# Recurrence gates as fp32r products, a later attention transpose and new pacing prices in a two-layer encoder trunk

## The chip, the cores and the metric

One core of one Trainium2 chip runs the whole kernel in one launch. The metric is device time in microseconds; a measurement is the median of several runs. The engines are named as the profile names them: PE (matrix products), DVE (vector), ACT (activation), POOL (GpSimd) and SP (which issues most transfers). They run side by side, each takes its own instructions in order, and they meet through semaphores.

## The reference

Two layers work on a sequence of 512 tokens of width 1024. A layer first mixes tokens: the normalised input goes through one combined projection and feeds three branches (a gated 128-block mixing, a sparse attention with 128 selected keys per query, and a gated linear recurrence). The branches are projected, gated and summed, then projected once more and added to the stream. A convolutional feed-forward part follows in the same way. The change concerns the recurrence's two gates and the order of work in the attention:

```python
xc = causal_dwconv(xb, conv_w, conv_b)
xg = xc.reshape(bsz, seq, LRU_BLOCKS, LRU_BLOCK_DIM)          # 8 blocks of 64 channels
r = jax.nn.sigmoid(jnp.einsum('bsnc,ncd->bsnd', xg, w_r).reshape(bsz, seq, LRU_WIDTH) + b_r)
i = jax.nn.sigmoid(jnp.einsum('bsnc,ncd->bsnd', xg, w_i).reshape(bsz, seq, LRU_WIDTH) + b_i)
log_a = -LRU_C * r * jax.nn.softplus(-lam)
a = jnp.exp(log_a)
b = jnp.sqrt(-jnp.expm1(2.0 * log_a)) * (i * xc)
h = scan(a, b)                                                 # h[t] = a[t] h[t-1] + b[t]
```

## The kernel before

Everything lies with channels on the 128 partitions and the 512 tokens along the row. A dense product is a **unit**: one weight tile of 128 x 1024 is loaded from HBM by SP, split into a high part (ACT, a copy that rounds to fp32r) and a low part (DVE, a subtraction), and multiplied in three fp32r products per 128 rows (`mm3`, line 163: high by high, high by low, low by high), so 24 matmuls of 512 columns. `Stream.conv` (line 197) splits weights up to five units ahead (`LA`), through six staging buffers. The order of the units is a fixed list (`unit_names`, line 40): four `lx` (recurrence input), four `qi` and one `ki` (selection), `v`, `lg`, `gv`, `gu`, the recurrence's branch, four pairs `k`, `q`, the other two branches, then the output projection `wo` and the feed-forward units. In layer 0 the first seven units are computed in the program's head, in layer 1 the first five in the tail of the layer before; `col` (line 428) then only hands their results over (`carry`).

Beside the units run background tasks, written as generators. After each unit the program calls `B.pump` (line 247); each call is a **slot**. A task that yields a negative number sleeps so many slots. Tasks marked `must` run in every slot that they are due; the others (selection, and the `low` modulation sums) run only while the counter `work["v"]` (priced DVE work) is under `work["pe"]` (priced PE work) plus 2. `cost_v`, `cost_g` and `cost_t` (lines 109 to 119) hold the prices. All this decides only the order in which instructions are issued; nothing is reordered at run time.

The recurrence is `lru` (line 625), a `must` task added after the four `lx` slots. It sleeps three slots in layer 0, two in layer 1, then per slot computes the gates of one tile of 128 channels: two fp32 matmuls of 512 columns with block-diagonal weights (two blocks of 64 channels) on the convolved tile `xc[t]`, two sigmoids on ACT. Then come exponentials, square root, scan, and four slots later the products that the recurrence's branch takes (`get_yc`, line 985). The convolved tile is made in `layer` (lines 824 to 832): one ACT instruction and three DVE instructions per tile.

In the same slots the `qi` units get a rotation (`rope`, line 556: two ACT copies, one DVE and two POOL operations) and are split (`split_qi`, line 839: ACT, POOL, ACT); `place_low` (line 846) then moves low parts to other partitions by four SP transfers per tile.

Attention (`attention`, line 727) is a `must` task with one step per slot and 12 groups of query blocks. At step n it transposes group n-2 on PE (`flip`), multiplies group n-3 with the values, divides group n-1 on DVE, and scores group n (matmul, DVE reduction, ACT exponential). A head's first score waits for four slots after its `q` unit, and each group for its selection mask `bias[i]` (two slots after `ready[i]`). The result `yb` is taken by the third branch through `get_yb` (line 1009), which drains all tasks.

Of the kernel before, what the change touches and what calls it, by code (L numbers as in the profile page):

```python
# [16 lines left out]
P = 128  # L17
D = 1024
# [50 lines left out]
def trunk_kernel(ctx: ExitStack, tc: tile.TileContext, x, cc, wt, wf, wm, wu, cp, rows, gmw, gmb, lruw, cst, out):  # L69
# [44 lines left out]
    def cost_g(op, a):  # L114
        if op == "tensor_tensor":
            work["v"] += size(a[0]) * 0.0008
# [508 lines left out]
    def lru(l, xc, lw, s84, wts, gl, res):  # L625
        rr, ii = [], []
        yield -3 if l == 0 else -2
        for t in range(4):
            for wi_, ob, lst in ((0, O_BR, rr), (1, O_BI, ii)):
                p = bank()  # L630
                mm(p, wts[wi_][:, t * P:(t + 1) * P], xc[t], True, True)
                o = S()
                act(o, p, AF.Sigmoid, bias=lw[:, ob + t:ob + t + 1])
                lst.append(o)
            if t < 3:
                yield -1
# [90 lines left out]
    def attention(qk, at, v, bias, ready, res):  # L727
# [51 lines left out]
        for n in range(len(groups) + 3):  # L779
            if 2 <= n < len(groups) + 2:  # L780
                for pr in groups[n - 2]:
                    flip(*pr)
            if n >= 3:
                for pr in groups[n - 3]:
                    values(*pr)
            if 1 <= n <= len(groups):
                for pr in groups[n - 1]:
                    divide(*pr)
            if n < len(groups):
                for hd, i in groups[n]:  # L790
                    while len(qk) <= hd or B.slot < at[hd] + 4 or i not in bias or B.slot < ready[i] + 2:
                        yield -1
                    score(hd, i)
            yield 1.0
            yield -1
# [20 lines left out]
    def layer(l):  # L816
        lw, bg2, s84 = par.pop(l)
        B.low.append(mods([(l, 2, ("G", 0)), (l, 4, ("A", 1)), (l, 3, ("B", 1))]))
# [190 lines left out]
        def get_yb():  # L1009
            B.drain()  # L1010
            return yb
# [88 lines left out]
    def rstd0(q):  # L1100
        ts(q, q, D * EPS, None, AD)
        return rsqrt(q)
# [29 lines left out]
    ys[3] = rstd0(sumsq_v(3))  # L1132
    ys[2] = rstd0(q2)
    scale0(3, V)
    scale0(2, A_)
# [82 lines left out]
def lay_out(a):  # L1218
# [48 lines left out]
    for l in range(DEPTH):  # L1267
# [3 lines left out]
        c[:, O_BR:O_BR + 4] = cols(a["lru_b_r"][l])  # L1271
        c[:, O_BI:O_BI + 4] = cols(a["lru_b_i"][l])
# [19 lines left out]
    lruw = np.zeros((DEPTH, 2, P, 4, P), f)  # L1292
    for i, n in enumerate(("lru_w_r", "lru_w_i")):
        w = a[n].reshape(DEPTH, 4, 2, 64, 64)
        for e in range(2):
            lruw[:, i, e * 64:(e + 1) * 64, :, e * 64:(e + 1) * 64] = w[:, :, e].transpose(0, 2, 1, 3)
# [45 lines left out]
```

## Time and profile before

| | us |
|---|---|
| median of 3 runs (1716.35 to 1716.80) | 1716.53 |
| the profiled execution, its own time | 1715.37 |
| its span, first to last instruction | 1713.6 |
| PE busy | 1682.9 (98%) |
| DVE busy | 1139.0 (66%) |
| ACT busy | 698.7 (41%) |
| POOL busy | 258.8 (15%) |

Times are from the start of the span. Matmuls overlap in the pipeline: a row says 0.39 us for one whose successor starts 0.23 us later, so the pace is read from starts, and an idle time that a row names is what was left after the modelled end. `L106` is the line of the wrapper through which the priced instructions are issued, `L144` and `L139` those of ACT's copies and activations, so tiles (`ps`, `s`, `wh`, `wl`) tell what an instruction is. `ps<-s,s` on PE is a product of two working tiles (gates, scores, values), `ps<-ks,s` a transpose, `ps<-hh,wh` and the like a unit.

### The profile page before, as it was taken

The page shows a single profiled execution, that of the slowest core. Times are in us where ns is not written, and L with a number is a line of the kernel's source. Part 1 is how long each engine was busy: PE and PEld are TensorE (multiplying, and loading weights), DVE is VectorE, ACT ScalarE, POOL GpSimd, SP SyncE. Part 2 cuts the span into 40 slices and gives each one's busy share as a digit, 9 for nine tenths or more (in the row PEclk, how much of TensorE's full clock was granted, in tenths as well). Part 3 has the DMA queues.
Part 4 walks back from the last instruction along what each step waited for, and adds up shares of the span by engine and source line. Part 5 has one row for each costly group of instructions (what it writes and reads, how often), then busy time and mean ns, then how long its engine had stood idle before and what let it go on. Part 6 is the DMA issues. An engine that isn't in the chain of part 4 may idle for free.

```text
span 1713.6 us, 20805 instructions
## 1 busy us (share of the span) xinstructions
PE 1682.9 (98%) x7900; PEld 1399.4 (82%) x7900; DVE 1139.0 (66%) x1687; ACT 698.7 (41%) x1074; POOL 258.8 (15%) x231
## 2 busy tenths in 40 slices
PE   7999998999999999999999999989999999999998
PEld 6788886888888888888897888877888988888886
DVE  7778999674567787453566889886455686445442
ACT  6774234342344433332346632343333343333331
POOL 4400105110001311100004001141100011111000
PEclk9999999999999999999999999999999999999999
DMA  9542236552425665333155422564223354323311
GB/s 355 180 147 86 74 117 224 163 172 94 141 74 154 203 225 171 99 98 99 62 173 151 132 86 87 172 198 146 80 93 124 99 175 145 99 98 99 99 50 49
DMA packets 69896, 226.69 MB, mean 132 GB/s; under 512 B 8226, under 2 KB 9634, under 8 KB 69668
## 3 DMA queue, kind: packets, MB, share of 16 engines
q1 hardware_dynamic: 69504, 225.22, 40.6%
q8 instruction: 62, 1.02, 0.3%
q14 instruction: 38, 0.31, 0.1%
q10 hardware_dynamic: 292, 0.14, 0.0%
HBM read 219.03 MB, written 4.19 MB: 130 GB/s over the span
## 4 chain that ended last, share of the span: by engine, by line
PE 79%; DVE 14%; ACT 2%; issue 2%; DMA 2%; POOL 0%; SPq 0%; DVEq 0%; ACTq 0%; POOLq 0%
PE ps L106 79%; DVE s L106 7%; DVE wl L106 3%; DVE m L106 2%; DMA ms<-in_wm_dram 1%; DVE acc L106 1%; ACT wh L144 1%; DVE junk L106 1%; ACT s L139 0%; ACT s L144 0%; DVE sm L106 0%; DMA x<-in_x_dram 0%; POOL sm L106 0%; ACT hh L144 0%; DMA m<-in_wt_dram 0%
## 5 line engine op out<-in xcount | busy, mean ns | idle before, releaser
L106 PE MATMUL ps<-hh,wh 128*128 128x512 f32 (+1 forms) x1608 | 608.9, 379 | 1.0 <-ACT s L144 0.9
L106 PE MATMUL ps<-hl,wh 128*128 128x512 f32 (+1 forms) x1608 | 601.3, 374 | 2.7 <-DVE hl L106 2.7
L106 PE MATMUL ps<-hh,wl 128*128 128x512 f32 (+1 forms) x1608 | 601.0, 374 | 0.0
L106 DVE TENSOR_TENSOR wl<-wst,wh 128x1024 fp32r<-128x1024 f32 x271 | 359.1, 1328 | 239.9 <-ACT wh L144 239.6
L144 ACT ACTIVATE wh<-wst 128x1024 fp32r<-128x1024 f32 x271 | 284.5, 1054 | 192.0 <-PE ps L106 188.3
L106 PEld LDWEIGHTS ps<-hl,wh 128*128 128x128 f32 x1608 | 303.3, 189 | 59.6 <-DVE hl L106 4.0
L106 PEld LDWEIGHTS ps<-hh,wh 128*128 128x128 f32 x1608 | 303.4, 189 | 57.6 <-issue 1.9
L106 PEld LDWEIGHTS ps<-hh,wl 128*128 128x128 f32 x1608 | 303.1, 188 | 53.9
L106 POOL TENSOR_TENSOR s<-s,s 128x512 f32<-128x512 f32 (+1 forms) x102 | 171.5, 1689 | 658.7 <-DVE s L106 543.8
L106 PE MATMUL ps<-wh,s 128*128 128x512 f32 x832 | 261.3, 390 | 0.0
L106 DVE SCALAR_TENSOR_TENSOR s<-ps,lw,s 128x511 f32<-128x511 f32 (+3 forms) x208 | 154.1, 748 | 136.0 <-ACT s L139 132.4
L139 ACT ACTIVATE s<-ps,lw 128x512 f32<-128x512 f32 x112 | 84.0, 764 | 259.0 <-PE ps L106 259.0
L106 PEld LDWEIGHTS ps<-wh,s 128*128 128x128 f32 x832 | 156.2, 188 | 32.1
L106 PE MATMUL ps<-wl,s 128*128 128x512 f32 x416 | 161.9, 389 | 0.0
L106 PE MATMUL ps<-s,s 128*128 128x512 f32 (+3 forms) x608 | 129.5, 357 | 1.5 <-ACT s L144 1.5
L106 PE MATMUL ps<-s,wh 128*128 128x512 f32 x384 | 121.1, 397 | 0.0
L106 PEld LDWEIGHTS ps<-s,s 128*128 128x128 f32 x608 | 93.1, 191 | 15.8 <-issue 3.1
L106 DVE SCALAR_TENSOR_TENSOR acc<-ms,cact,acc 128x1024 f32<-128x1024 f32 x70 | 93.3, 1333 | 13.9 <-DMA ms<-in_wm_dram 13.9
L106 POOL TENSOR_TENSOR sm<-sm,mhalf 128x1 f32<-128x1 f32 x40 | 22.5, 565 | 521.3 <-DVE sm L106 521.3
L139 ACT ACTIVATE s<-ps,bg 128x512 f32<-128x512 f32 x48 | 33.0, 687 | 151.9 <-PE ps L106 151.9
L106 PEld LDWEIGHTS ps<-wl,s 128*128 128x128 f32 x416 | 78.1, 188 | 16.2
L106 PEld LDWEIGHTS ps<-s,wh 128*128 128x128 f32 x384 | 71.8, 188 | 17.2 <-issue 2.9
(105 smaller groups left out, 1416.3 us busy)
## 6 DMA issues: line engine op xcount, KB each, us to landing
wst<-in_wu_dram SPq DMA_DIRECT2D x279, 512.0 KB, 3.7
ms<-in_wm_dram SPq DMA_DIRECT2D x80, 512.0 KB, 4.4
s<-in_rows_dram SPq DMA_DIRECT2D x34, 256.0 KB, 5.8
m<-in_wt_dram SPq DMA_DIRECT2D x16, 512.0 KB, 6.1
x<-in_x_dram SPq DMA_DIRECT2D x4, 512.0 KB, 5.8
s<-in_wf_dram SPq DMA_DIRECT2D x8, 256.0 KB, 6.7
s<-s SPq DMA_DIRECT2D x32, 64.0 KB, 3.0
s<-in_x_dram SPq DMA_DIRECT2D x8, 256.0 KB, 5.6
```

Source lines behind the costliest of these rows:

```text
L106: return f(*a, **k)
L139: A_.activation(o, i, f, bias=bias, scale=scale)
L144: A_.activation(o, i, AF.Copy, scale=scale)
```

## The change

The gates of a tile come from two products of another make-up. The tile `e` holds the rounded input of block A (rows 0 to 63) and, in rows 64 to 127, the low part of block A; `o` the same for block B with the halves exchanged. The weights of both gates stand side by side, so one result holds both gates of one block; per block one matmul takes the high weights and one the low weights, whose rows for the low input are set to zero. The low parts get to the other rows by transfers (`place`), and three more transfers per tile (`join`) put the gates of both blocks into order again. The work runs in six slots from the second slot on: splits of tile t, two slots later its gates. The host lays out weights and biases accordingly.

Besides, a POOL `tensor_tensor` costs more in the pacing, the counter is clamped when a layer starts, `flip` and `values` come one step later, `get_yb` pumps only until `yb` is there, and in the head the norm of token block 2 is computed on POOL and scaled on DVE.

```diff
     def cost_g(op, a):
         if op == "tensor_tensor":
-            work["v"] += size(a[0]) * 0.0008
+            work["v"] += size(a[0]) * 0.0018
...
     def lru(l, xc, lw, s84, wts, gl, res):
-        rr, ii = [], []
-        yield -3 if l == 0 else -2
-        for t in range(4):
-            for wi_, ob, lst in ((0, O_BR, rr), (1, O_BI, ii)):
-                p = bank()
-                mm(p, wts[wi_][:, t * P:(t + 1) * P], xc[t], True, True)
-                o = S()
-                act(o, p, AF.Sigmoid, bias=lw[:, ob + t:ob + t + 1])
-                lst.append(o)
-            if t < 3:
-                yield -1
+        rr, ii, xs, low, ge = [], [], [], [], []
+        yield -1
+        wh, wl = [], []
+        for e in range(2):
+            a, c = S(F32R), S(F32R)
+            split(a, c, wts[e])
+            z = slice(64, P) if e == 0 else slice(0, 64)
+            G_.memset(c[z].bitcast(F32), 0.0)
+            wh.append(a)
+            wl.append(c)
+        wts = None
+        def place():
+            for e, o, c in low:
+                nc.sync.dma_start(e[64:P].bitcast(F32), c[0:64].bitcast(F32))
+                nc.sync.dma_start(o[0:64].bitcast(F32), c[64:P].bitcast(F32))
+            del low[:]
+        def join():
+            for a, c in ge:
+                i = S()
+                nc.sync.dma_start(i[0:64], a[64:P])
+                nc.sync.dma_start(i[64:P], c[0:64])
+                nc.sync.dma_start(a[64:P], c[64:P])
+                rr.append(a)
+                ii.append(i)
+            del ge[:]
+        for t in range(4 + 2):
+            if t >= 2:
+                g = []
+                for e in range(2):
+                    p = bank()
+                    ws = slice((t - 2) * P, (t - 1) * P)
+                    mm(p, wh[e][:, ws], xs[0][e], True, False)
+                    mm(p, wl[e][:, ws], xs[0][e], False, True)
+                    o = S()
+                    ob = (O_BR, O_BI)[e] + t - 2
+                    act(o, p, AF.Sigmoid, bias=lw[:, ob:ob + 1])
+                    g.append(o)
+                xs.pop(0)
+            place()
+            if t < 4:
+                e, o, c = S(F32R), S(F32R), S(F32R)
+                split(e, c, xc[t])
+                copy(o, xc[t])
+                low.append((e, o, c))
+                xs.append((e, o))
+            yield -1
+            join()
+            if t >= 2:
+                ge.append(g)
+        yield -1
+        join()
+        yield -1
...
-        for n in range(len(groups) + 3):
-            if 2 <= n < len(groups) + 2:
-                for pr in groups[n - 2]:
+        for n in range(len(groups) + 4):
+            if 3 <= n < len(groups) + 3:
+                for pr in groups[n - 3]:
                     flip(*pr)
-            if n >= 3:
-                for pr in groups[n - 3]:
+            if n >= 4:
+                for pr in groups[n - 4]:
                     values(*pr)
...
         lw, bg2, s84 = par.pop(l)
+        work["v"] = min(work["v"], work["pe"])
...
         def get_yb():
-            B.drain()
+            while None in yb:
+                B.pump(True)
             return yb
...
-    ys[3] = rstd0(sumsq_v(3))
-    ys[2] = rstd0(q2)
+    ys[2] = rstd0(q2, G_)
+    q3 = sumsq_v(3)
+    scale0(2, V)
+    ys[3] = rstd0(q3)
     scale0(3, V)
-    scale0(2, A_)
```

## Rows read from the trace of the kernel before

**Rows 1.** The page, part 1: busy time and share of the span by engine.

```profile
PE 1682.9 (98%) x7900; PEld 1399.4 (82%) x7900; DVE 1139.0 (66%) x1687; ACT 698.7 (41%) x1074; POOL 258.8 (15%) x231
```

**Rows 2.** Timeline of PE, layer 1: start, duration, instruction, count [idle before, releaser].

```profile
904.74 0.39 PE L106 MATMUL ps<-hh,wl 128*128 128x512 f32 x1
...
906.33 1.88 PE L106 MATMUL ps<-s,s 128*128 128x512 f32 x4
```

**Rows 3.** Stages: length, busy time (count) by engine, granted clock, DMA. Layer 0, gates.

```profile
64.17:71.38 7.21, 7.21 (x30) 5.26 (x29) 5.21 (x8) 1.63 (x3) 2.87 (x3) 1.00 0.09 35
...
78.78:87.80 9.02, 7.47 (x29) 5.18 (x28) 4.76 (x4) 6.06 (x9) 5.89 (x4) 1.00 0.74 223
```

**Rows 4.** Timeline of PE, layer 0, third tile of the gates.

```profile
81.35 1.12 PE L106 MATMUL ps<-s,s 128*128 128x512 f32 x2 [1.55 <-ACT s L144]
```

**Rows 5.** Stages: first attention steps of both layers, then two later units.

```profile
276.88:297.05 20.17, 14.99 (x57) 10.98 (x56) 17.61 (x30) 9.13 (x19) 10.34 (x7) 0.83 0.74 240
1123.41:1143.26 19.85, 15.23 (x56) 11.12 (x55) 16.73 (x28) 9.35 (x18) 10.20 (x7) 0.83 0.58 174
299.45:305.10 5.65, 5.65 (x26) 4.62 (x25) 5.48 (x13) 0.67 (x3) 2.27 (x2) 1.00 0.45 143
306.56:312.35 5.79, 5.79 (x26) 4.62 (x25) 4.83 (x10) 2.94 (x6) 0.00 (x0) 1.00 0.66 202
```

**Rows 6.** Timeline of DVE, layer 0, first attention steps.

```profile
281.00 0.28 DVE L106 CUSTOM_DVE_ANT_0 s<-ps,bias 128x128 f32<-128x128 f32 x1
...
287.35 1.30 DVE L106 TENSOR_SCALAR s<-s,sm 128x256 f32<-128x256 f32 x1
```

**Rows 7.** Timeline of PE, layer 0, the first transposes of the attention.

```profile
287.39 0.45 PE L106 MATMUL ps<-ks,s 128*128 128x128 f32 x1 [4.22 <-DVE sm L106]
```

**Rows 8.** Stages: the stretches of lower granted clock in both layers.

```profile
285.42:292.24 6.82, 3.89 (x8) 2.35 (x9) 6.11 (x11) 3.35 (x6) 2.35 (x2) 0.50 0.59 175
...
1131.93:1138.74 6.81, 4.42 (x10) 2.74 (x11) 5.30 (x13) 3.42 (x8) 2.35 (x2) 0.50 0.30 93
```

**Rows 9.** Timeline of PE, layer 0, first tile of the gates.

```profile
64.17 1.88 PE L106 MATMUL ps<-s,s 128*128 128x512 f32 x4
```

**Rows 10.** Timeline of DVE, layer 0: the convolution, three ropes.

```profile
58.70 8.99 DVE L106 SCALAR_TENSOR_TENSOR s<-ps,lw,s 128x511 f32<-128x511 f32 x12
67.61 1.88 DVE L106 TENSOR_TENSOR s<-ps,ks 128x512 f32<-128x512 f32 x3
```

**Rows 11.** Groups by line, shapes apart: busy, mean ns of one | idle before.

```profile
L106 DVE TENSOR_TENSOR s<-s,s 128x512 fp32r<-128x512 f32 x62 | 45.5, 747 | 3.0 <-ACT s L144 3.0
...
L106 POOL MEMSET s<- 128x512 f32 x2 | 1.0, 520 | 0.0
```

**Rows 12.** Timeline of DVE beside a busy POOL, layer 0.

```profile
270.37 1.77 DVE L106 TENSOR_TENSOR s<-acc,s 128x512 fp32r<-128x512 f32 x1
```

**Rows 13.** Timeline of POOL, layer 0, ropes of the selection units.

```profile
68.43 1.29 POOL L106 TENSOR_TENSOR s<-s,s 128x512 f32<-128x512 f32 x1 [6.20 <-DVE s L106]
69.69 1.09 POOL L106 TENSOR_TENSOR s<-s,ks 128x512 f32<-128x512 f32 x1
...
72.10 2.08 POOL L106 TENSOR_TENSOR s<-s,ks 128x512 f32<-128x512 f32 x1
```

**Rows 14.** Transfers of line 849 (place_low): time from issue to landing.

```profile
DMA to landing us min/median/max: 1.9/3.2/5.6
```

**Rows 15.** Timeline of SP, layer 0: place_low.

```profile
77.68 0.58 SPq L849 DMA_DIRECT2D s<-s  x1
```

**Rows 16.** Timeline of DVE, layer 1: the convolution, second rope.

```profile
894.85 8.98 DVE L106 SCALAR_TENSOR_TENSOR s<-ps,lw,s 128x511 f32<-128x511 f32 x12
...
905.48 0.68 DVE L106 TENSOR_TENSOR s<-ps,ks 128x512 f32<-128x512 f32 x1
```

**Rows 17.** Timeline of POOL, layer 1: last rope step and low part.

```profile
912.55 3.50 POOL L106 TENSOR_TENSOR s<-s,s 128x512 f32<-128x512 f32 x2
```

**Rows 18.** Timeline of SP, layer 1: place_low.

```profile
916.08 0.52 SPq L849 DMA_DIRECT2D s<-s  x1
```

More of the change, by code (lines that the diff above doesn't have):

```diff
@@ new lines, in join @@
+        def join():
[27 more added lines that the diff above has]
+                xs.append((e, o))
+                e = o = c = None
+            yield -1
+            join()
+            if t >= 2:
+                ge.append(g)
+                g = o = None
@@ L637, in lru @@
+        yield -1
+        join()
+        wh = wl = None
+        yield -1
         while l not in prepared:
@@ L1098, in dot, with rstd0 @@
         V.tensor_tensor_reduce(junk2[:, :n], a, b, 1.0, 0.0, M, AD, o)
-    def rstd0(q):
-        ts(q, q, D * EPS, None, AD)
+    def rstd0(q, eng=None):
+        ts(q, q, D * EPS, None, AD, eng=eng)
         return rsqrt(q)
@@ L1270, in lay_out @@
         c[:, O_CB:O_CB + 4] = cols(a["lru_conv_b"][l])
-        c[:, O_BR:O_BR + 4] = cols(a["lru_b_r"][l])
-        c[:, O_BI:O_BI + 4] = cols(a["lru_b_i"][l])
+        br, bi = cols(a["lru_b_r"][l]), cols(a["lru_b_i"][l])
+        c[:, O_BR:O_BR + 4] = np.concatenate([br[:64], bi[:64]])
+        c[:, O_BI:O_BI + 4] = np.concatenate([bi[64:], br[64:]])
         c[:, O_LAM:O_LAM + 4] = cols(a["lru_lam"][l])
@@ L1291, in lay_out @@
     gmb = a["gm_b_s"].reshape(DEPTH, 512)
-    lruw = np.zeros((DEPTH, 2, P, 4, P), f)
+    lruw = np.zeros((DEPTH, 2, 2, 64, 4, 2, 64), f)
     for i, n in enumerate(("lru_w_r", "lru_w_i")):
@@ L1295, in lay_out @@
         for e in range(2):
-            lruw[:, i, e * 64:(e + 1) * 64, :, e * 64:(e + 1) * 64] = w[:, :, e].transpose(0, 2, 1, 3)
+            lruw[:, e, :, :, :, i ^ e] = w[:, :, e].transpose(0, 2, 1, 3)[:, None]
     lruw = lruw.reshape(DEPTH, 2, P, 512)
```

## The prediction

> **What bounds the kernel now.** I read the page's first part, then the stages, then the places where the matmul engine stops. PE is busy for 98% of the span and DVE for 66% [rows 1]. Busy hides gaps inside a pipelined stream, so the pace has to be read from a stage: in an ordinary stretch matmuls start every 0.227 us (906.33 less 904.74 is seven starts [rows 2]), and a weight unit of 24 costs 5.44 us. Most stages run at that pace. So the program ends when PE's list ends; a microsecond taken from PE's list is a microsecond won, and work on DVE, ACT, POOL or SP costs nothing until a matmul waits for it.
>
> Three places are off the pace. The recurrence gates: one tile's gates and the next unit take 7.21 us [rows 3], so the gates cost 7.21 - 5.44 = 1.77 us per tile. The third tile of layer 0 takes 9.02 us [rows 3], because a matmul stood 1.55 us behind ACT [rows 4]: sigmoids lagged, and it probably found no free PSUM bank. And the first attention steps: from the second score to the fourth step takes 20.17 us in layer 0 and 19.85 in layer 1 [rows 5], against 5.65 and 5.79 for the same two units later on [rows 5], plus 1.1 for two scores and three transposes (by their columns, two passes each, at the pace of rows 2): 12.6. Each layer loses 7.6 or 7.3 us there. The cause is on DVE: the first scores are reduced from 281.00 on and divided by 288.65 [rows 6], and the transposes (`flip`), whose turn came 4.2 us earlier, at 283.2, start at 287.39 [rows 7]. After that gap the granted clock is 0.50, the lower of the two levels (1.2 GHz), for 6.8 us in both layers [rows 8]; in layer 0 4.9 us of it lie behind the restart, which costs about 2.5 us (it is in the 7.6 and 7.3).
>
> **The change, part by part.** I sum against the profiled execution (1715.37 us; span 1713.6). The median of the runs is 1.16 us above it, and I add that at the end.
>
> (a) Gate matmuls. Sixteen fp32 matmuls (two passes each) become 32 fp32r ones. Old: 8 tiles x 1.77 = 14.2. New: 8 x 4 x 0.227 = 7.3. Gain 6.9.
>
> (b) The attention lag. `flip` moves one step back, so every transpose gets one more slot (a unit and a score, 5.8 us) after its divide was issued. The late divide ended at 288.65 [rows 6]; without the stop PE comes to it at 283.2 (287.39 less the idle 4.22 [rows 7]) + 0.46 + 5.44 = 289.1. That suffices even if DVE stays as late as now. It will be less late: the price of a POOL operation in the pacing goes from 0.41 to 0.92 us, and about 29 POOL operations are issued in a layer before step 2 (10 for the qi and ki ropes, 4 low parts, 4 of the mix, 11 or 12 of the k and q ropes), so some 15 us of paced DVE work (selection, modulation) is issued later against PE. Adding up the counters slot by slot, the selection's last part in layer 0 moves from about the 33rd slot to the 40th, where step 2 (slot 42) just takes it; attention ends at slot 56 instead of 55, and its user comes after slot 57. The modulation sums move into the branch stage, where DVE has room. `get_yb` waits only for yb, which nothing reaches. I take the whole 14.9 as gained; the other bound is half (one layer still stops).
>
> (c) The first gate of layer 0. This is the change's price. Today it needs only the convolved tile, ready near 61 (three of the twelve DVE steps [rows 10]), and runs at 64.17 [rows 9]. Its place in PE's list stays (behind the fourth qi unit), but now it waits for weights split in two, for a tile split in two, and for a transfer of the low part. All of that is queued on DVE behind the 12 convolution steps (until 67.6) and two ropes, so it starts at 68.8 [rows 10]. Two weight splits and one tile split follow: 0.75 us each in the mean of such operations, 1.77 in a place where POOL also works [rows 11, 12]. POOL is busy from 68.43 without a break [rows 13]; I take 1.2 each, so the low part exists at 72.4. A transfer of this kind lands 1.9 to 5.6 us after its issue, 3.2 in the median [rows 14]: about 75.4. PE idles 64.2 to 75.4, 11.2 us, and nothing else is in its list. With the lower clock behind it (2.5) this costs 13.7; bounds: 0.75 each and a landing of 1.9 give 8.8 + 2.5 = 11.3, 1.77 each and 5.6 give 15.5 + 2.5 = 18. The bank stop at the third tile goes, as ACT catches up meanwhile: gain 1.8.
>
> (d) The second gate of layer 0. Its transfers stand on SP behind the four of `place_low`, which wait for POOL's low part of the first qi tile. SP issues those from 77.68 on today, 0.6 us apart [rows 15]. POOL gets two memsets (0.52 each [rows 11]) and is held up by the new splits; I put `place_low` 3 us later, the gate's transfer behind its four at 83.2 and its landing at 86.2. PE comes there at 75.4 + 0.9 + 5.4 + 2.5 = 84.2. Cost 2; bounds 0 and 4.
>
> (e) The same in layer 1. The gates move from the third qi unit to the fourth (906.33 to about 911.8). Convolution ends at 903.8, the second rope at 906.1 [rows 16]; three splits at 1.2 give 909.7, landed 912.8: the first gate costs 1. For the second, POOL's seven operations ended at 916.05 today [rows 17] and `place_low` began at 916.08 [rows 18]. With memsets and splits I take 917.6, the four issues until 920.1, then the gate's transfer, landed 923. PE is there at 911.8 + 1 + 0.9 + 5.4 = 919.1, so it idles 3.9 us, about as long as the stop of rows 7, and I count the clock again: 3.9 + 2.5 = 6.4 (bounds 0 and 8). Together 7.4.
>
> (f) At nothing: 12 more transfers per layer for joining, on SP (under 0.6 us each, with the weight stream five units ahead); ten more ACT copies per layer, on an engine busy for 41% [rows 1]; the recurrence's tail, later by two to four slots but done some three slots before its user, the branch that takes it; the new order of the first norms (one scaling goes from ACT to DVE, and a power follows sooner on POOL: one delay against another, plus or minus 0.4); the clamp of the pacing counter at a layer's start, which the lower bound of the counter overrides at the first pump.
>
> Sum: -6.9 - 14.9 + 13.7 - 1.8 + 2 + 7.4 = -0.5. From the median: 1716.53 - 0.5 = 1716.0 us. What the two repairs win is paid back at the gates.
>
> On the splits' price a page speaks against the change. The rows show a POOL operation nearly doubling when it meets a DVE split (1.09 to 2.08 [rows 13]). The Trainium skill, "SBUF — State Buffer", section "SBUF: two separate sides", says that the pair of ports they share is an exclusive lock held for a whole instruction. By that each split would wait out a whole POOL operation, and the sum would be that of the second rival below, 8 us on the slow side instead of -0.5.
>
> **Rivals.** *Faster: the second gates find their data.* If POOL meets DVE less often (its operations take 1.09 to 1.29 alone [rows 13], and the modulation sums that met it in layer 1 are now held back), `place_low` stays near today's time and the second gates cost 0: terms (d) and the 6.4 fall away, and the sum is -8.9, 1707.6 us. For it: the POOL operations of layer 0 up to 72 were short [rows 13]; against it: DVE has three splits more just there. Chance 0.36.
>
> *Slower: POOL and DVE shut each other out.* If each split waits for a whole POOL operation (0.7 + 1.2 instead of 1.2), the first low part is 2 us later in both layers. In layer 1 the first gate then idles 3 us, and there the clock falls once more (2.5): +2 + 2 + 2.5. POOL's own chain, held by the splits, delays both second gates by 1 more. Sum -0.5 + 8.5 = 8.0, 1724.5 us. It decides from the point where the layer-1 low part exists later than about 911. Chance 0.20.
>
> *The change does not do what it says.* If DVE's lag, and not the one slot, is what counts, a transpose of a later step waits in its turn and the stop only moves: half of 14.9 stays, sum 7.0, 1723.5 us. Against it: after the stop today, DVE keeps up with the old order in the steps that follow [rows 5]. Chance 0.06.
>
> **The numbers.** The sum itself, within 0.2%, has 0.38. A measurement of this kernel tells 0.2% (3.4 us) from no change. So faster 0.36, within 0.38, slower 0.26. The likeliest case alone spans 1712 to 1720. The range takes in the rivals' values and leaves out the far ends of (c): 1705.5 to 1725.
>
> **What would show it.** Right: in layer 0 PE idle for some 11 us before the first gate, released by a transfer, and the granted clock at 0.50 around it; a shorter stop before the second gate in each layer, also released by a transfer; no stop over 1 us in the first attention steps, and PE's clock at 1.00 there; gate matmuls 0.23 us apart instead of 0.44. Wrong: a first gate of layer 0 that runs before 72, a transpose that still waits for DVE, or a PE stop in a place not named here, such as the user of yb or the start of the output projection.

## The result, and the profile after

The changed kernel takes 1728.62 us (median of 4 runs, 1727.34 to 1729.99), the kernel before 1716.66 in the same session: a ratio of 1.0069, interval 1.0052 to 1.0087. It is slower by 12.0 us, against a forecast of 1716.0 and outside its range. The span grew by the same 12.0 us (1713.6 to 1725.6).

PE is still busy nearly throughout. The groups below, from part 5 of the page of the changed kernel, stand against [rows 1]: PE's products of two working tiles now wait, mostly for transfers, and the modulation sums on DVE wait for their weights (13.9 us in that group before, 27.7 now).

```profile
PE 1679.7 (97%) x7900; PEld 1399.2 (81%) x7900; DVE 1150.0 (67%) x1699; ACT 718.0 (42%) x1099; POOL 258.3 (15%) x236
...
L106 PE MATMUL ps<-s,s 128*128 128x512 f32 (+3 forms) x608 | 125.3, 348 | 22.7 <-DMA s<-s 14.2
...
L106 DVE SCALAR_TENSOR_TENSOR acc<-ms,cact,acc 128x1024 f32<-128x1024 f32 x70 | 91.6, 1308 | 27.7 <-DMA ms<-in_wm_dram 27.7
```

The timeline of PE in the changed kernel (start, duration, instruction, count, idle before and its releaser) at the gates of both layers, at the first score of each layer, and wherever PE stood longer than 0.9 us in the token-mixing part:

```profile
76.03 2.05 PE L106 MATMUL ps<-s,s 128*128 128x512 f32 x4 [11.58 <-DMA s<-s]
...
84.78 1.08 PE L106 MATMUL ps<-s,s 128*128 128x512 f32 x4
...
282.64 0.92 PE L106 MATMUL ps<-s,s 128*128 128x128 f32 x4 [0.74 <-POOL s L106]
...
312.04 2.11 PE L106 MATMUL ps<-s,s 128*128 128x128 f32 x8 [3.58 <-ACT s L144]
...
506.06 0.28 PE L106 MATMUL ps<-hh,wh 128*128 128x256 f32 x1
...
923.27 1.40 PE L106 MATMUL ps<-s,s 128*128 128x512 f32 x4 [0.98 <-DMA s<-s]
...
931.82 1.37 PE L106 MATMUL ps<-s,s 128*128 128x512 f32 x4 [1.67 <-DMA s<-s]
...
973.39 0.79 PE L106 MATMUL ps<-s,s 128*128 128x384 f32 x3 [3.20 <-ACT s L139]
...
1130.71 0.81 PE L106 MATMUL ps<-s,s 128*128 128x128 f32 x4
...
1150.58 0.44 PE L106 MATMUL ps<-ks,s 128*128 128x128 f32 x2 [0.99 <-DVE s L106]
...
1161.49 0.55 PE L106 MATMUL ps<-ks,s 128*128 128x128 f32 x3 [2.83 <-ACT s L144]
...
1354.25 0.28 PE L106 MATMUL ps<-hh,wh 128*128 128x256 f32 x1
```

The same four marks (first score, end of the token part, in each layer) in the timeline of PE of the kernel before:

```profile
270.76 0.82 PE L106 MATMUL ps<-s,s 128*128 128x128 f32 x4
...
495.71 0.28 PE L106 MATMUL ps<-hh,wh 128*128 128x256 f32 x1
...
1117.29 0.82 PE L106 MATMUL ps<-s,s 128*128 128x128 f32 x4
...
1342.30 0.28 PE L106 MATMUL ps<-hh,wh 128*128 128x256 f32 x1
```

Subtracting marks cuts the 12 us into four stretches:

| stretch | forecast | measured |
|---|---|---|
| layer 0 to the first score: half of (a), (c), (d) | -3.45 + 13.7 - 1.8 + 2 = +10.45 | 282.64 - 270.76 = +11.9 |
| layer 0, attention and what follows: (b) | -7.6 | 223.42 - 224.95 = -1.5 |
| layer 1 to the first score: half of (a), (e) | -3.45 + 7.4 = +3.95 | 624.65 - 621.58 = +3.1 |
| layer 1, attention and what follows: (b) | -7.3 | 223.54 - 225.01 = -1.5 |

Up to the first score each layer costs what was forecast, within a microsecond and a half. The attention gained 3.0 us where 14.9 were expected, 11.9 of the 12.5 us by which the forecast missed. These marks say where the time is, not what took it: part of what the attention lacks may come from the gates (all_but_gates, below).

Where the attention's gain went is in the stages of the changed kernel (length, busy time and count of PE, PEld, DVE, ACT, POOL, granted clock, DMA share, GB/s): the first gate's half clock, the two stretches of [rows 5] (second score to step 3), and the two steps behind each of them.

```profile
76.03:80.96 4.93, 4.93 (x12) 3.84 (x13) 4.93 (x4) 4.86 (x7) 4.93 (x3) 0.50 0.69 227
288.87:301.36 12.49, 12.49 (x54) 9.71 (x53) 12.28 (x21) 3.24 (x7) 6.34 (x5) 1.00 0.34 119
1136.83:1149.32 12.49, 12.49 (x54) 9.67 (x52) 10.79 (x19) 5.71 (x11) 5.99 (x5) 1.00 0.69 230
301.36:320.60 19.24, 15.66 (x67) 12.23 (x66) 15.21 (x33) 11.62 (x23) 5.13 (x4) 0.91 0.44 138
1149.32:1169.74 20.42, 15.48 (x71) 11.74 (x71) 17.18 (x30) 9.98 (x20) 6.17 (x5) 1.00 0.56 177
```

The steps that took 20.17 and 19.85 us now take 12.49 in both layers, as forecast (12.6). But the next two steps take 19.24 and 20.42, where an undisturbed pair takes 13.60 (a row further down): the stop moved two steps on. DVE is busy for 12.28 of 12.49 us in layer 0: there nothing has made it less late. The chain behind the stop of 3.58 us, from the timelines of DVE and then ACT of the changed kernel:

```profile
294.50 0.28 DVE L106 CUSTOM_DVE_ANT_0 s<-ps,bias 128x128 f32<-128x128 f32 x1
...
307.72 0.68 DVE L106 CUSTOM_DVE_ANT_0 s<-ps,s 128x512 f32<-128x512 f32 x1
...
308.71 0.72 ACT L141 ACTIVATE s<-s,sm 128x512 f32<-128x512 f32 x1 [3.34 <-DVE sm L106]
...
309.43 1.04 ACT L144 ACTIVATE wh<-wst 128x1024 fp32r<-128x1024 f32 x1
310.50 1.77 ACT L144 ACTIVATE s<-ps 64x512 f32<-64x512 f32 x4
```

The first scores, made at 282.64, are reduced on DVE at 294.50, 11.9 us later (before: 281.00 [rows 6] less 270.76, 10.2). The fourth score, made at 295.01, is reduced at 307.72; ACT's exponential waits for it; behind it on ACT stand a weight split, two copies of a rotation, and only then the copies of the transposes that step 4's values need. In layer 0 the transposes no longer wait, but their copy does; in layer 1 two transposes still wait 0.99 us for DVE, and three stand 2.83 us behind ACT. The Trainium skill, "Perfetto Trace Analysis", section "Tensor Engine Instruction (MATMUL, LD_WEIGHTS)", calls ACT and DVE strict FIFO; these rows agree.

### The profile page after: what moved, and what is told of

It is laid out like the page before. It is cut to its first block, busy times and chain, and to the rows that moved or that the text cites. A ratio compares the mean times of both kernels' runs of the same rounds, so it can differ in the third digit from the quotient of the medians.

```text
span 1725.6 us, 20944 instructions
## 1 busy us (share of the span) xinstructions
PE 1679.7 (97%) x7900; PEld 1399.2 (81%) x7900; DVE 1150.0 (67%) x1699; ACT 718.0 (42%) x1099; POOL 258.3 (15%) x236
## 4 chain that ended last, share of the span: by engine, by line
PE 80%; DVE 12%; ACT 3%; issue 2%; DMA 1%; POOL 1%; SPq 0%; DVEq 0%; ACTq 0%; POOLq 0%
PE ps L106 80%; DVE s L106 7%; DVE wl L106 3%; DVE m L106 1%; ACT s L139 1%; ACT wh L144 1%; ACT s L144 1%; DVE junk L106 0%; DVE sm L106 0%; ACT L139 0%; POOL sm L106 0%; DMA x<-in_x_dram 0%; DMA wst<-in_wu_dram 0%; POOL s L106 0%; DMA s<-s 0%
## 5 line engine op out<-in xcount | busy, mean ns | idle before, releaser
L106 PE MATMUL ps<-s,s 128*128 128x512 f32 (+3 forms) x608 | 125.3, 348 | 22.7 <-DMA s<-s 14.2
L106 DVE SCALAR_TENSOR_TENSOR acc<-ms,cact,acc 128x1024 f32<-128x1024 f32 x70 | 91.6, 1308 | 27.7 <-DMA ms<-in_wm_dram 27.7
L106 DVE TENSOR_TENSOR s<-s,s 128x512 fp32r<-128x512 f32 (+2 forms) x120 | 89.8, 765 | 11.2 <-ACT s L144 10.1
L144 ACT ACTIVATE s<-ps 64x512 f32<-64x512 f32 (+6 forms) x110 | 59.0, 546 | 80.4 <-PE ps L106 77.9
```

The costliest lines, as they stand in the source:

```text
L106: return f(*a, **k)
L144: A_.activation(o, i, AF.Copy, scale=scale)
```

## The experiments

Theories, numbered as in the expectations: (1) pacing: the new price puts the selection in front of the first scores; (2) recurrence: the gates' extra work makes DVE and ACT late; (3) the new attention order is worth nothing; (4) SP's order: the joining transfers hold up the modulation's weights; (6) collision: the recurrence's part on ACT meets the selection's scores.

### The parts, alone and undone

**before_gates_new** is the kernel before with the new gates (`lru` and the host layout of the diff), nothing else. **before_attention_new** is the kernel before with the new order and `get_yb`:

```diff
-                B.drain()
+                while None in yb: B.pump(True)
...
-                for pr in groups[n - 2]:
+                for pr in groups[n - 3]:
                     flip(*pr)
...
-                for pr in groups[n - 3]:
+                for pr in groups[n - 4]:
                     values(*pr)
```

**before_price_new** has only `* 0.0018` for `* 0.0008` in `cost_g`. **after_price_old** and **after_attention_old** are the changed kernel with the price, and the order in `attention`, put back.

Expected, before_gates_new: 

> The kernel before with only the new gates and their host layout. Theory 1 (pacing): the gates cost what they cost in the changed kernel, 8.8 us in layer 0 up to the v unit and about 3 in layer 1, and the attention stops of before stay as they are: about 1728.5 us, or 1725.3 if the stop of 3.2 us at 970 belongs to the price. Theory 2 (recurrence): DVE's lag at the first scores grows past 11 us and the stops at the transposes with it: 1732 us or more.

Expected, before_attention_new: 

> The kernel before with only the new order of attention (transposes in step 3, values in step 4) and the shorter wait for its results. Theory 1 (pacing): with the old price the lag of DVE is as in the rows of before, one more slot covers it, and both stops go: 1716.7 - 14.9 = 1701.8 us, no stop over 1 us in the first attention steps. Theory 3 (the stop only moves): half or less is gained, 1709 to 1717 us, with a stop at step 4 behind ACT's copy of the transposes.

Expected, before_price_new: 

> The kernel before with only the price of a POOL operation raised to 0.0018. By the prediction's step on pacing, less paced work lies ahead of the first scores, so the stops at the transposes (4.2 and 3.6 us, with the clock worth 14.9) shorten: 1709 to 1714 us. Theory 6 (the price only moves the selection later, towards the first scores): the same stops or longer ones, 1716 to 1722 us.

Expected, after_price_old: 

> The changed kernel with the price of a POOL operation in the pacing back at 0.0008. Theory 1 (pacing): the higher price makes the selection of the keys run late, so on DVE it stands ahead of the first scores (reduced 11.9 us after PE made them, 282.64 to 294.50, where it was 10.2 us before), and the stop of the first attention steps only moves from the transposes to step 4. With the old price the stops of 3.6 us at 308 and of 1.0, 2.8 and 0.8 us from 1149 to 1163 go, and the lower clock of 313 to 316 (3.4 us, worth 1.7) with them: 1728.6 - 3.6 - 1.7 - 4.6 = about 1718.7 us. Theory 2 (recurrence): DVE is late because the recurrence has more work there and ends later; the price has little part: 1727 to 1730 us, the same stops. The stop of 3.2 us at 970, behind ACT's share of the recurrence, stays by both.

Expected, after_attention_old: 

> The changed kernel with the transposes back in step 2 and the values in step 3. Theory 1 (pacing): DVE is later than before, so the transposes wait longer than the 4.2 and 3.6 us of before, by about the 1.7 us by which the scores are reduced later; with the lower clock behind it each layer loses some 9 instead of its present 5: about 1736 us. Theory 3 (the order is worth nothing, the stop only moves): 1726 to 1731 us.

| kernel | median, us | ratio to before, interval |
|---|---|---|
| before_gates_new | 1744.15 | 1.0164 (1.0150 to 1.0178) |
| before_attention_new | 1712.94 | 0.9978 (0.9969 to 0.9987) |
| before_price_new | 1710.38 | 0.9964 (0.9951 to 0.9977) |
| after_price_old | 1741.84 | 1.0146 (1.0132 to 1.0160) |
| after_attention_old | 1734.66 | 1.0106 (1.0092 to 1.0120) |

The gates alone cost 27.7 us. Their first wait is the one of the changed kernel (11.57 us), but PE also stands 7.18 us at the first score of layer 0 (behind POOL's rotation), 3.21 at the selection's scores of layer 1 (behind ACT), and 4.16 and 6.23 us at the transposes; the price, taken back, costs 13.2 us; and the new order gains 3.5 us alone and 6.0 in the changed kernel. So theory 1 fell: the price does not cause the loss, it hides half of it (neither theory had 1741.84 for after_price_old). Theory 2's 1732 us or more was met by before_gates_new. Theory 3 fell as an absolute, but most of the forecast gain of the order is missing even without the gates. The price alone gains 6.3 us: the stop of layer 1 shrank from 3.60 to 1.38 us, that of layer 0 stayed (4.25). That part of step (b) held for one layer. No run has the new order and the new price together without the gates and with the modulation sums where they were.

Why the order gains so little stands in before_attention_new, PE and then DVE:

```profile
293.13 0.82 PE L106 MATMUL ps<-s,s 128*128 128x256 f32 x2 [2.36 <-DVE s L106]
296.07 0.80 PE L106 MATMUL ps<-hh,wh 128*128 128x512 f32 x1 [2.12 <-DVE sm L106]
...
1146.98 2.29 PE L106 MATMUL ps<-s,s 128*128 128x128 f32 x7 [3.56 <-ACT s L144]
```

```profile
292.38 0.69 DVE L106 TENSOR_TENSOR s<-ps,ks 128x512 f32<-128x512 f32 x1
...
295.32 0.68 DVE L106 CUSTOM_DVE_ANT_0 s<-ps,s 128x512 f32<-128x512 f32 x1
```

In layer 0 PE goes on at 293.13 and 296.07, right as DVE ends an instruction that reads a PSUM bank (292.38 + 0.69, 295.32 + 0.68). Each score and each unit holds a bank until DVE has read it, so PE probably found no free bank; that reading comes from the times of the rows, and no run changed the number of banks. In layer 1 it is ACT's copy again. Both are the same lag of DVE, met one or two steps later.

### What keeps DVE late at the attention

**attention_new_mods_held** adds to before_attention_new a pause of the modulation sums (`B.low`), from the `k`, `q` units to attention's step 5; **after_mods_held** puts the same into the changed kernel:

```diff
-            if self.low and not carry and free():
+            if self.low and not carry and not self.quiet and free():
...
+            if n == 5:
+                B.quiet = False
             yield 1.0
...
         B.add(attention(qk, at, v, bias, ready, yb), True, must=True)
+        B.quiet = True
```

**mods_held_attention_later** moves after_mods_held's first score of a head from four slots behind its `q` unit to six (`B.slot < at[hd] + 6`).

Expected, attention_new_mods_held: 

> The kernel before with the new order of attention (1712.9 us: stops of 2.4 and 2.1 us at 290 and 293, of 0.8 and 3.6 us at 1142 and 1143, each with the lower clock behind it), and with the modulation sums held back from the start of the k and q units to attention's step 5. In that kernel PE goes on when DVE frees a PSUM bank, so it runs no further ahead of DVE than the banks last. If the modulation sums make DVE late: the stops shrink below 1 us and the clock stays up: 1716.7 - 14 = about 1703 us. If the selection and the weights do: 1710 to 1714 us.

Expected, after_mods_held: 

> The changed kernel with the modulation sums held back until attention's step 5, the edit that took 13 us off the kernel with the new attention order alone. If the modulation sums are what keeps DVE late there too: the stops of 3.6 us at 308 and of 1.0, 2.8 and 0.8 us from 1149 to 1163 go, with 1.7 of half clock: about 1718.5 us. If here the selection does it (the price has moved it up to the first scores): at most a third of that, 1724 to 1728 us.

Expected, mods_held_attention_later: 

> The changed kernel with the modulation sums held (1725.1 us) and attention's first score two slots later (some 11 us of PE). In layer 0 that kernel still stops 3.6 us at 308, with 6.8 us of half clock behind, and no modulation sum runs there any more: on DVE the last part of the selection stands ahead of the first scores. If that is the cause: the later scores meet an idle DVE, the stops at 282 (0.7) and 308 go, and with them up to 2.4 of half clock: 1718.5 to 1721 us. Rival (once late, DVE and ACT hold each other: the exponentials wait for DVE, DVE for weights that ACT splits behind them): the stop moves two slots on, 1724 to 1727 us.

Measured: attention_new_mods_held 1699.67 us (1699.62 to 1699.73), ratio 0.9903 (0.9890 to 0.9917). All stops of the attention are gone, and with them the lower clock: these are the stages from the second score to step 3 and from there to step 5.

```profile
276.69:289.18 12.49, 12.49 (x54) 9.71 (x53) 9.05 (x17) 5.50 (x11) 5.09 (x4) 1.00 0.27 85
289.18:302.78 13.60, 13.60 (x67) 11.22 (x66) 7.97 (x21) 7.44 (x15) 2.45 (x2) 1.00 0.25 80
```

DVE is busy for 9.05 of 12.49 us here instead of 12.28 in the changed kernel, and it reduces the first score of layer 0 3.1 us after PE made it (270.57, 273.69; 10.2 us in the kernel before). So in the kernel before it is the modulation sums that keep DVE behind PE. The two edits together gain 16.5 us, more than the 14.9 of the forecast. How much of that the new order still adds is open, as no run holds the sums with the old order. The rows let one expect little: DVE's first divides now end at 280.77, before PE comes to the step in which the old order had its transposes (282.82), and in layer 1 at 1121.32, before 1122.07.

```profile
279.45 1.32 DVE L106 TENSOR_SCALAR s<-s,sm 128x256 f32<-128x256 f32 x1
```

```profile
282.82 1.02 PE L106 MATMUL ps<-s,s 128*128 128x512 f32 x2
```

In the changed kernel the same edit gives 1725.06 us (ratio 1.0046, 1.0033 to 1.0059), as the second expectation says: the stops of layer 1 are gone, that of 3.58 us in layer 0 stays to the hundredth. There DVE still works on the selection: its last MAX8 begins at 285.11 in the changed kernel, behind the first score, where the kernel before had it at 243.58. In mods_held_attention_later (1726.03 us, ratio 1.0049, 1.0036 to 1.0061) the scores come two slots later; neither stop of layer 0 is left, the clock is 1.00 from 282.64 to 313.00, and the rival (a convoy that moves along) fell by its mechanism, though the time lies in its range. The first expectation's mechanism did not come either: the scores did not meet an idle DVE, the first still waits 10.1 us (293.00 to 303.07), and what is gone by the time that the transposes need ACT is the rotations' copies (the last end at 308.1). That the selection makes the lag is read from DVE's rows and from after_gate_later (below), where the first score comes at 287.14, behind the last MAX8 (285.31): it waits 4.9 us, and the stop of 3.58 is not there. The time did not fall, as near the layer's end PE stood 4.90 us for a modulation sum, probably because it had been held too long:

```profile
458.79 1.52 PE L106 MATMUL ps<-s,onesr 128*128 128x512 f32 x2 [4.90 <-ACT s L144]
```

### What the gates do behind their own wait

In the changed kernel `join` issues three transfers per tile; the third overwrites what the first reads, so SP stands for the first. **after_join_later** issues the third in the next slot; **after_price_old_join_later** does so at the old price:

```diff
         def join():
+            for a, c in late:
+                nc.sync.dma_start(a[64:P], c[64:P])
+                rr.append(a)
+            del late[:]
             for a, c in ge:
                 i = S()
                 nc.sync.dma_start(i[0:64], a[64:P])
                 nc.sync.dma_start(i[64:P], c[0:64])
-                nc.sync.dma_start(a[64:P], c[64:P])
-                rr.append(a)
                 ii.append(i)
+                late.append((a, c))
```

Expected, after_join_later: 

> The changed kernel with the third of the three joining transfers of a tile issued one slot later. It overwrites what the first one reads, and in the changed kernel SP stands for it 4 to 5 us per tile (33.2 us in 8 waits), with the modulation's weights behind it. Theory 4 (SP's order): SP's wait there falls below 3 us, DVE's waits for the modulation's weights fall from 38.8 us towards the 15.3 of before, and the stop of 3.2 us at 970, where ACT stood behind such a wait of DVE (8.5 us), goes; the attention stops change little: 1722 to 1725.5 us. Theory 2 (the amount of new work on DVE and ACT): the stops stay, 1727.5 to 1730 us.

Expected, after_price_old_join_later: 

> The same shift of the third joining transfer, in the changed kernel with the old price of a POOL operation (1741.8 us, DVE waiting 52.4 us for the modulation's weights). Theory 4 (SP's order): the stops of 8.5 us at 128 and 3.2 us at 984 go, with the lower clock behind the first (10.2 us at half clock, of which the stop covers most): about 1728 us, so most of what the old price costs is SP's blocking, met at an earlier place. Theory 2 (the amount of new work): 1738 to 1742 us.

Measured: 1727.78 us (ratio 1.0068, 1.0055 to 1.0081) and 1737.90 (1.0125, 1.0110 to 1.0140). The wait did go; these are SP's own waits at that transfer, first in the changed kernel, then in after_join_later (engine, line, what for: us in total, times, longest):

```profile
SPq L651 <- DMA s<-s: 33.2, 8, 4.8
```

```profile
SPq L648 <- DMA s<-s: 5.2, 3, 2.8
```

DVE's waits for the modulation's weights fell from 38.8 to 23.3 us, and yet PE's stops stayed, 3.20 us at 974 and 3.58 in the attention. So theory 4 explains at most 3.9 us of these two kernels, at the old price, where 7.42 of the 8.53 us of the stop stayed. What stops PE there is ACT's order. In after_price_old, PE and then ACT:

```profile
137.16 1.33 PE L106 MATMUL ps<-s,s 128*128 128x384 f32 x3 [8.53 <-ACT s L139]
```

```profile
128.10 1.28 ACT L139 ACT_TABLE_LOAD   x1
129.39 2.84 ACT L139 ACTIVATE s<-s,s 128x512 f32<-128x512 f32 x4
132.25 1.28 ACT L139 ACT_TABLE_LOAD   x1
134.66 2.19 ACT L139 ACTIVATE s<-s 128x512 f32<-128x512 f32 x4 [1.12 <-DVE s L106]
136.75 5.15 ACT L139 ACTIVATE s<-ps 128x256 f32<-128x256 f32 x14
```

The selection's scores start at 126.29, probably fill their banks, and wait for ACT's ReLUs (136.75), which stand behind the recurrence's exponentials (129.39) and roots (134.66) with two table loads. In the kernel before that work was over some 19 us ahead of the scores: its last root ended at 103.8 (in ACT's timeline, 101.65 + 2.19), its first score product began at 122.8. In the changed kernel the same meeting, with the exponentials and one table load, is the 3.20 us at 973.39. Four runs tried to take it apart.

**after_gate_later** puts the gates of a tile four slots behind its split in layer 0, three in layer 1 (`range(4 + L)`, `t >= L`). **price_old_scores_wait** is the changed kernel at the old price with the scores held behind the roots, **mods_held_scores_wait** the same on after_mods_held with one slot, **combined** the old price, held scores, later gates and held sums at once:

```diff
             act(rr[t], rr[t], AF.Sqrt)
+        rooted.append(l)
...
-            yield -1
+            while l not in rooted:
+                yield -1
+            yield -2
             yield from indexer(qi, kih, wr_.pop(), bias, ready)
```

Expected, after_gate_later: 

> The changed kernel with the gates of a tile four slots behind its split in layer 0 (two before) and three in layer 1; nothing else moves. If the first gate's wait is the price of the change: PE's idle of 11.6 us before it shrinks to about 1, the half clock behind it (worth 2.4) goes, and so do the 1.0 and 1.7 us in layer 1: 1728.6 - 10.6 - 2.4 - 2.6 = 1713.0 us. Rival (the recurrence, now ending later, meets its user): a new stop where ACT takes the selection's scores or where the branch takes the recurrence, and less than half is gained: 1721 us or more.

Expected, price_old_scores_wait: 

> The changed kernel with the old price (1741.8 us) and one edit: the selection's score matmuls are held until two slots after the recurrence has issued its square roots. Theory 6 (collision on ACT): the new gates end the recurrence's exponentials and roots on ACT where the selection's scores wait for ACT to empty their banks (roots until 136, scores from 128 on), and all that the higher price does against that is to move the scores away. Then the stops of 8.5 us at 128 and 3.2 at 984 go, with most of the 10.2 us of half clock behind the first (worth up to 5): 1725 to 1730 us. Theory 4 (SP and the modulation's weights): the recurrence itself is late, the stops only move: 1736 us or more.

Expected, mods_held_scores_wait: 

> The changed kernel with the modulation sums held (1725.1 us) and the selection's score matmuls held until one slot after the recurrence has issued its roots. In layer 0 that is so already; in layer 1 the scores come at 968, and ACT, in order, has 4.1 us of the recurrence's exponentials and a table load ahead of them. If the collision on ACT is the cause: the stop of 3.2 us at 971 goes, with most of the 6.8 us of half clock behind it (worth up to 2.4), and the selection, later in layer 1 now, has room since the sums are held there: 1720 to 1722.5 us. Rival (the scores only meet the next group on ACT or DVE, as in the kernel with the old price): 1725 us or more, with a stop behind DVE in the selection of layer 1.

Expected, combined: 

> The changed kernel with the old price, the scores held until after the roots, the gates four (layer 0) and three slots (layer 1) behind their splits, and the modulation sums held back until attention's step 5. If the three causes (first gate, collision on ACT, modulation sums ahead of attention) are all there is: the 1699.7 us of the kernel with the new attention order and held sums, less 6.9 for the gates and 1.5 for the old bank stop, plus 2.4 for what the later gates still waited (0.7 and 1.7 us): about 1693.7 us. If the gates keep a price of their own (the later recurrence meets the branch that takes it, or the selection meets attention): 1700 us or more.

| kernel | median, us | ratio to before, interval | what went | what came |
|---|---|---|---|---|
| after_gate_later | 1724.46 | 1.0047 (1.0034 to 1.0059) | 11.58 at the first gate (0.73 left), 3.58 in the attention of layer 0 | 13.76 behind ACT |
| price_old_scores_wait | 1745.91 | 1.0174 (1.0160 to 1.0189) | 8.53 behind ACT | 7.42 behind POOL |
| mods_held_scores_wait | 1727.50 | 1.0060 (1.0048 to 1.0073) | 3.20 behind ACT | 4.88 behind POOL |
| combined | 1749.29 | 1.0192 (1.0178 to 1.0206) | the first gate, 8.53 | 12.18, 10.06 and 12.12 |

PE's longest new stop, one fence per kernel in the order of the table:

```profile
142.81 0.80 PE L106 MATMUL ps<-s,s 128*128 128x256 f32 x2 [13.76 <-ACT s L139]
```

```profile
288.13 1.22 PE L106 MATMUL ps<-s,s 128*128 128x128 f32 x3 [7.42 <-POOL s L106]
```

```profile
1134.86 1.65 PE L106 MATMUL ps<-s,s 128*128 128x128 f32 x4 [4.88 <-POOL s L106]
```

```profile
172.93 0.58 PE L106 MATMUL ps<-s,s 128*128 128x256 f32 x1 [12.18 <-DVE wi L106]
```

Theory 6 holds for the stop: separating the two groups removes it in both layers. It fell for the time: the selection then starts later, ends in front of the attention on DVE, and PE stands at the first score for a rotation whose DVE part is late (288.13, 1134.86). In after_gate_later (1724.46 us, in its rival's range) the scores start earlier, at 127.95 instead of 164.26, and meet the recurrence. Most of that stop is not ACT's own work: the roots end it at 142.50 after waiting 8.46 us for DVE, and DVE had stood 9.41 us for a modulation's weights:

```profile
133.98 1.29 DVE L106 SCALAR_TENSOR_TENSOR acc<-ms,cact,acc 128x1024 f32<-128x1024 f32 x1 [9.41 <-DMA ms<-in_wm_dram]
```

SP stood 12.2 us for the joining transfers between 100 and 140 there, so theory 4 may have a part in this kernel; no run has the later gates with the later join. combined changes four things, and which of them makes each of its stops was not tried.

### The gates as the rest

**all_but_gates** is after_mods_held with `lru` and the layout as before; price, attention, head and clamp stay new.

Expected, all_but_gates: 

> The changed kernel with the modulation sums held (1725.1 us) and the gates and their layout as before: price, attention order, head and clamp new. If the gates alone carry the loss: as fast as the kernel before with the new order and held sums, 1699.7 us, within 2, so the new gates cost 25 us here. Rival (the price or the head costs something of its own): 1703 us or more.

Measured: 1700.35 us (1700.07 to 1700.57), ratio 0.9903 (0.9888 to 0.9918), 0.7 us from attention_new_mods_held. So price, head and clamp change less than a microsecond together there, and the gates cost 24.7 us in that kernel, not the 14.4 that the terms (a), (c), (d), (e) and the bank stop add up to. The four marks of the two kernels (271.56, 489.16, 1109.82 and 1327.47; with the gates 282.93, 507.48, 1134.39 and 1352.00) put +11.4 us of it up to the first score of layer 0, +7.0 into the attention of layer 0 and what follows, +6.3 up to the first score of layer 1, and nothing behind it. The 7.0 us are mainly the stop of 3.58 and the lower clock behind it (0.61 on the mean over the next 7.69 us). The fastest version is attention_new_mods_held, 16.5 us under the kernel before and 29 under the changed one.

## Why the prediction was wrong

**(b), the step that failed.** "That suffices even if DVE stays as late as now" looked at one consumer, the transpose, and at one wait, the divide. In layer 0 the transposes did run without a stop, but their copies on ACT, the values behind them and probably the scores' PSUM banks depend on the same lag of DVE, and the stop reappeared two steps on. Measured -3.0 us, not -14.9; alone, with DVE as late as before, -3.5 (before_attention_new). "It will be less late" held for layer 1 and not for layer 0: with the price alone the first score of layer 0 waits 10.07 us for DVE (270.77 to 280.84 in before_price_new), hardly less than the 10.2 of before, as the modulation sums still stand ahead of it. In the changed kernel it waits 11.9 us and the selection stands ahead of it: its last MAX8 begins at 243.58 in the kernel before, at 249.82 with the price alone, at 269.71 with the gates alone and at 285.11 with both. The rival "the change does not do what it says" had the mechanism, lag and not one slot; its price (half of 14.9 stays) was too small, some 12 of it stayed, and its chance of 0.06 was far too low. The evidence cited against it (DVE keeps up after the stop) was taken behind a stop that had let DVE catch up.

**(a)**: right in layer 0, where the second tile's four matmuls take 0.92 us without a stop (84.78 to 85.70); in layer 1 they took 1.24 and 1.20 for the first two tiles (923.27 to 924.51, 931.82 to 933.02), so a little of the 6.9 was not won.

**(c)**: the sum was right, in part by luck. PE idled 11.58 us (forecast 11.2) until 76.03 (75.4), then ran 4.93 us at a granted clock of 0.50, worth 2.5. The three splits took longer than the 1.2 us each (until 73.57, forecast 72.4), and the transfer, issued at 73.60, landed sooner than its 3 us.

**(d), (e)**: too high. The second gate of layer 0 found its data; in layer 1 the gates waited 0.98 (forecast 1) and 1.67 us (3.9), and the clock stayed up: 2.65 us, not 7.4. The faster rival (the second gates find their data) was thus right in layer 0 and mostly in layer 1, but it counted all of (b) as gained. That two steps erred in the good direction hid an error in (f).

**(f)**: the recurrence's tail was put at nothing as it was "done some three slots before its user". The user was not the point: its exponentials, roots and table loads are in ACT's order, and the next to need ACT was the selection. 3.20 us here, 8.53 at the old price. Besides, the attention of layer 0 costs 7.0 us more with the gates where the sums are held (after_mods_held against all_but_gates); the rows put this down to the selection, which comes later behind the recurrence, but no run moved it by itself. The joins did hold up SP (33.2 us), which hardly mattered here (after_join_later). Head and clamp at nothing were right within a microsecond (all_but_gates), but the reason given for the clamp was wrong: the counter's lower bound can only raise it, so it cannot override a clamp that lowers it.

**The rival of exclusive ports** asked for a first gate in layer 1 that idles 3 us, with the lower clock behind it. It idled 0.98 at full clock. Yet its mechanism is in the rows. The first two of the three splits of layer 0 on DVE, then POOL's operations beside them, in the changed kernel:

```profile
68.96 1.44 DVE L106 TENSOR_TENSOR s<-s,s 128x512 fp32r<-128x512 f32 x1
70.32 1.58 DVE L106 TENSOR_TENSOR s<-s,s 128x512 fp32r<-128x512 f32 x1
```

```profile
68.59 1.26 POOL L106 TENSOR_TENSOR s<-s,s 128x512 f32<-128x512 f32 x1 [6.21 <-DVE s L106]
69.81 1.54 POOL L106 TENSOR_TENSOR s<-s,ks 128x512 f32<-128x512 f32 x1
```

Each split ends 0.55 us after the POOL operation that was running when it began (70.40 behind 69.85, 71.90 behind 71.35; the third, 1.75 us long, 73.57 behind 73.03), as if it had waited for that one's end. This agrees with the whole-instruction lock that the Trainium skill's page "SBUF — State Buffer" describes in its section "SBUF: two separate sides". What was too high is the rival's price: a split waited only for what was left of an operation, 1.44 to 1.75 us in all instead of 1.9. No run here tried it by itself.

**What would show it** worked: "a PE stop in a place not named here" came true, at the values and at the selection's scores, and so did "a transpose that still waits for DVE", in layer 1 (0.99 us).

## What to carry to other kernels

When an engine that runs behind is the cause of a stop, moving the consumer by a step only helps if the lag is shorter than every later buffer and queue allows: follow the lag through the copies, banks and in-order engines behind the consumer, or take work off the late engine, as held sums did. In a tight schedule of in-order engines, moving a group later can cost nothing at its user and much at the group it newly stands in front of; ask of each engine it touches who is next. A gain counted at full and a cover called free deserve the same bounds from both sides as a cost.

## What the hardware showed that was not expected

The same stop is not always followed by the lower clock. The 3.20 us at the selection's scores of layer 1 left the granted clock at 1.00 in the changed kernel and took it to half for part of the next stretch in after_mods_held, as these two stages behind the stop show (first the changed kernel):

```profile
973.39:981.00 7.61, 7.61 (x36) 6.45 (x37) 6.67 (x14) 6.59 (x19) 0.30 (x1) 1.00 0.73 245
```

```profile
974.83:981.40 6.57, 6.57 (x21) 6.36 (x22) 5.73 (x13) 5.61 (x16) 0.30 (x1) 0.57 0.71 229
```

21 matmuls start in 6.57 us there, 36 in 7.61 here. So a stop of this length has two prices. That would also fit the spread of after_mods_held (1721.60 to 1725.74), while the two kernels whose longest stop behind the head is 1.55 us repeat within 0.1 us (attention_new_mods_held) and 0.5 us (all_but_gates).

In the rows of after_price_old above, a change of ACT's table cost the load alone: 1.28 us, and the next activation began 0.01 us behind it (128.10 + 1.28, then 129.39); the load at 132.25 began 0.02 us behind the exponentials (129.39 + 2.84). The Trainium skill, "ScalarE: Activation LUTs", section "What ACT_TABLE_LOAD costs", gives 1.28 us for the load, which agrees, and some 1.4 us for a drain beside it, which these rows do not show.
